# Output projection of a hybrid decoder block: four parts of 512-column matmuls in place of two sweeps of 256-column matmuls

## The chip, the cores and the metric

The kernel runs on one core of a Trainium2 chip. The metric is the device time of one execution in microseconds (us); lower is better. TensorE (PE) multiplies matrices, VectorE (DVE), ScalarE (ACT) and GpSimd (POOL) do the rest, and SyncE (SP) issues nearly all DMA transfers, one after the other, from one queue.

## The reference

One decoder layer over 2048 tokens of width 1024: a norm, one input projection, three branches that read it, and one output projection that is added to the input. Widths: attention 512 (8 heads of 64), SSD 1024 (16 heads, two groups), LRU 512. All in float32.

```python
u = rms_norm(h, norm_g[l])
proj = jnp.einsum('bsd,de->bse', u, w_in[l])
(q, k, v, z_att, f_raw, z_ssd, xbc, dt_raw, x_lru, z_lru) = jnp.split(proj, split_points, axis=-1)
y_att = fox_attention(...) * jax.nn.silu(z_att)     # causal softmax with a forget bias
y_ssd = ssd_mixer(...)                              # its RMS norm: per token and group of 512
y_lru = rglru_mixer(...) * jax.nn.silu(z_lru)
mix = jnp.concatenate([y_att, y_ssd, y_lru], axis=-1)        # 512 + 1024 + 512 = 2048
h = h + jnp.einsum('bse,ed->bsd', mix, w_out[l])             # (2048 x 2048) by (2048 x 1024)
```

## The kernel before, in words

Every large product is made of three matmuls: both operands are split into a high part (fp32r) and the rest, and high x high, high x low and low x high are summed in PSUM. So weights are loaded ("wr", "wor"), copied to a high tile by ACT, and the low tile is made by VectorE as the difference.

The stages follow one another, and the framework's scheduler fixes at build time the order of instructions on each engine and on SP's queue, from each instruction's priority (its place in the program, moved up inside `high_priority`) and its own estimate of when operands and buffers are ready. `issue_after(x)` keeps the instructions of a block behind x on the same engine.

1. u, the normed and transposed input, is kept in SBUF split (`uh`, `ul`: four blocks tb of 512 tokens, 8 + 8 tiles of 2 KB per partition each, 128 KB in all). Projections of x/B/C, LRU, z and the SSD scan run first; branch outputs go to DRAM (`gt_d` for SSD, `lr_d` for LRU).
2. For four pairs of heads: Q and K are projected and normed, then `group_vz` projects V and the attention gate, eight steps t2 of two token tiles, 48 matmuls of 256 columns each. Three PSUM banks ("pj") hold their results. After the last pair, the pools of this phase, u among them, are closed (`pb.close()`), and the pools of the next phase take their place in SBUF and PSUM.
3. Attention: 64 units (head h, block sb of 256 queries). Heads 0 and 7 go from the longest block down, the others up. `logits` makes S = QK (L814, L815), VectorE subtracts the bias and keeps a running maximum (L816), ACT takes the exponential (L820). `attend` transposes the weights (T, L869) for each pair of key tiles, ACT and VectorE split them (ph L876, pl L877), and TensorE multiplies by V (O, L855, L856). Logits of the next unit are made within the present one. There are 288 transposition steps in all, and after each, `fill` takes steps of another job, the output projection, from a generator: `count * 512 // 288` steps so far, each allowed on TensorE after the transposition LAG = 4 steps back.
4. Output projection in two sweeps over 16 row tiles t. `load_wo` loads eight row tiles of w_out (512 KB each) and splits them in pieces of 512 columns: 16 pieces on ACT and VectorE. The first sweep takes w_out's rows 8 to 15 (SSD group 1 and LRU) and goes over t upwards, the second rows 4 to 7 (SSD group 0) and 0 to 3 (attention) and goes downwards. `mix(t)` loads the branch outputs of one tile ("mt"), makes "mh" on ACT (L956, for attention after four transposes px, L948) and "ml" on POOL (L957; for attention VectorE, L949); it is called a whole tile ahead. For each quarter n of 256 columns a PSUM tile `po` of two halves, one for each part, takes 8 x 3 matmuls of 256 columns (L977, L979, L981), with a `yield` ahead of each three: 16 x 4 x 8 = 512 steps a sweep. VectorE then adds each half to "xr" (L985, scaled for SSD by its norm `rsn`; L988), and xr is stored after two quarters.

The first sweep is the filler of attention: it reads x and writes the sum to `pt_d` in DRAM, with one PSUM bank (psP). The second sweep begins after attention, with five banks for `po` and three for px; it reads `pt_d` and writes the output. Weights of both sweeps have a pool of their own, 64 KB per partition: the first set is loaded after u's pools are closed, the second set after the filler's last step.

Of the kernel before, what the change touches and what calls it, by code (L numbers as in the profile page):

```python
# [29 lines left out]
QB = 5  # L30
ZPOOL = True
# [13 lines left out]
def hybrid_block(ctx, tc, x, norm_g, w_in, q_norm_g, k_norm_g, forget_b, ssd_conv_w, ssd_conv_b,  # L45
# [110 lines left out]
    up = pb.enter_context(tpool(name="up", bufs=1))  # L156
# [147 lines left out]
    def proj_tok2(w, t2, name, space=None):  # L304
# [3 lines left out]
        for i in range(2):  # L308
            t = t2 * 2 + i
            h, l, sl = uh[t // 4], ul[t // 4], slice(t % 4 * P, t % 4 * P + P)  # L310
            for k in range(KD):
                T.matmul(ps[:, i, :], h[k][:, sl], wh[k], start=(k == 0), stop=False)  # L312
                T.matmul(ps[:, i, :], h[k][:, sl], wl[k], start=False, stop=False)  # L313
                T.matmul(ps[:, i, :], l[k][:, sl], wh[k], start=False, stop=(k == KD - 1))  # L314
        return ps

# [11 lines left out]
    def group_vz(pool, vpool, p):  # L328
# [4 lines left out]
        for t2 in range(8):  # L333
# [5 lines left out]
            else:  # L339
                pss = [proj_tok2(w, t2, f"pvz{p}_{t2}")]  # L340
            m = 2 // len(pss)
# [386 lines left out]

    with tpool(name="ap", bufs=2) as pool, tpool(name="ap1", bufs=1) as ap1, \
            tpool(name="qkp", bufs=QB) as qkp:  # L730
        for p in range(4):
# [39 lines left out]
            if p == 2:  # L771
                load_head(0)
                load_q(*units[0])
    pb.close()
# [3 lines left out]
    o2 = cx.enter_context(tpool(name="o2", bufs=2))  # L778
    a2 = cx.enter_context(tpool(name="a2", bufs=2))
    a3 = cx.enter_context(tpool(name="a3", bufs=3))  # L780
    wo = cx.enter_context(tpool(name="wo", bufs=1))
    o1 = cx.enter_context(tpool(name="o1", bufs=1))
# [120 lines left out]
    def load_wo(ks):  # L903
        w = {}
        for j, k in enumerate(ks):
            h = wo.tile([P, D], F32R, name=f"woh{k}", tag=f"woh{j}")
            l = wo.tile([P, D], F32R, name=f"wol{k}", tag=f"wol{j}")
            row = w_out[k * P:(k + 1) * P, :]
            if j < 7:
                whole = wo.tile([P, D], F32, name=f"wor{k}", tag=f"wol{j + 1}")  # L910
                dma(whole, row)
            for n in range(2):
                cs = slice(n * 512, n * 512 + 512)
                if j < 7:
                    raw = whole[:, cs]
                else:
                    raw = o1.tile([P, 512], F32, name=f"wor{k}_{n}", tag=f"mt{n}")
                    dma(raw, row[:, cs])
                if 4 <= k < 12:
                    g = c1("sg", k - 4)  # L920
                    A.activation(h[:, cs], raw, AF.Copy, scale=g)
                    V.scalar_tensor_tensor(l[:, cs], raw, g, h[:, cs].bitcast(F32),
                                           op0=ALU.mult, op1=ALU.subtract)
                else:
                    A.copy(h[:, cs], raw)
                    V.tensor_tensor(l[:, cs], raw, h[:, cs].bitcast(F32),
                                    op=ALU.subtract)
            w[k] = (h, l)
        return w

    def sweep(w, psP, psX, parts, resid, dst, ts):


        ks = [k0 + i for _, k0 in parts for i in range(4)]

        def mix(t):
            tsl = slice(t * P, (t + 1) * P)
            mh = o2.tile([P, 8, P], F32R, name=f"mh{t}_{ks[0]}", tag="mh")
            ml = o2.tile([P, 8, P], F32R, name=f"ml{t}_{ks[0]}", tag="ml")
            for j, (kind, k0) in enumerate(parts):  # L940
                sl = slice(j * 4, j * 4 + 4)
                mt = o1.tile([P, 4, P], F32, name=f"mt{t}_{k0}", tag=f"mt{j}")
                if kind == "att":
                    dma(mt.rearrange("p i c -> p (i c)"), at_d[tsl, :])
                    src = psX.tile([P, 4, P], F32, name=f"px{t}_{k0}", tag="X")
                    for i in range(4):
                        T.transpose(src[:, i, :], mt[:, i, :], ident)  # L947
                    A.copy(mh[:, sl, :], src)  # L948
                    V.tensor_tensor(ml[:, sl, :], src, mh[:, sl, :].bitcast(F32), op=ALU.subtract)  # L949
                    continue  # L950
                if kind == "lru":
                    for m in range(4):
                        dma(mt[:, m, :], lr_d[m][:, tsl])
                else:
                    dma(mt, gt_d[kind][:, :, tsl].rearrange("i p t -> p i t"))
                A.copy(mh[:, sl, :], mt)  # L956
                G.tensor_tensor(ml[:, sl, :], mt, mh[:, sl, :].bitcast(F32), op=ALU.subtract)  # L957
            return mh, ml

        cur = mix(ts[0])  # L960
        for i, t in enumerate(ts):
            nxt = mix(ts[i + 1]) if i + 1 < NT else None
            tsl = slice(t * P, (t + 1) * P)
            mh, ml = cur
            for n in range(4):
                cs = slice(n * 256, n * 256 + 256)
                if n % 2 == 0:
                    xr = o2.tile([P, 512], F32, name=f"xr{t}_{n}_{ks[0]}", tag="xr")
                    dma(xr, resid[tsl, n * 256:n * 256 + 512])
                xc = xr[:, n % 2 * 256:n % 2 * 256 + 256]  # L970

                ps = psP.tile([P, 2, 256], F32, name=f"po{t}_{n}_{ks[0]}", tag="P")
                for j, k in enumerate(ks):
                    yield
                    h, l = w[k]
                    o = ps[:, j // 4, :]
                    T.matmul(o, mh[:, j, :], h[:, cs], start=(j == 0), stop=False,  # L977
                             skip_group_check=True)
                    T.matmul(o, mh[:, j, :], l[:, cs], start=False, stop=False,  # L979
                             skip_group_check=True)  # L980
                    T.matmul(o, ml[:, j, :], h[:, cs], start=False, stop=(j % 4 == 3),  # L981
                             skip_group_check=True)
                for j, (kind, _) in enumerate(parts):
                    if kind in (0, 1):
                        V.scalar_tensor_tensor(xc, ps[:, j, :], rsn[:, t, kind:kind + 1], xc,  # L985
                                               op0=ALU.mult, op1=ALU.add)
                    else:
                        V.tensor_tensor(xc, xc, ps[:, j, :], op=ALU.add)  # L988
                if n % 2:
                    dma(dst[tsl, n * 256 - 256:n * 256 + 256], xr)  # L990
            cur = nxt

    with tc.high_priority(offset=HP):
# [3 lines left out]
    w = load_wo(range(8, 16))  # L997
    filler = sweep(w, psP, None, ((1, 8), ("lru", 12)), xf, pt_d, range(NT))
# [54 lines left out]
```

## Time and profile before

| | |
|---|---|
| three runs | 2081.85, 2084.37, 2092.38 us (median 2084.37) |
| the profiled execution | 2094.4 us, its span 2092.4 us |
| TensorE busy | 2011.2 us (96%), mean granted clock 0.985 |
| VectorE, ACT, POOL busy | 61%, 46%, 26% |
| output projection, first sweep | first matmul at 1306.7 us, fills attention |
| attention | from about 1275 to 1893 us |
| output projection, second sweep | 1898 us to the end |
| DMA | 248.59 MB, mean 119 GB/s |

Times within the execution are counted from the span's start. A row of stretches gives busy microseconds of each engine in that stretch and, in brackets, how many instructions; "PEclk" is the share of full TensorE clock that was granted. A row of the order of time gives start and duration of an instruction, and in square brackets how long its engine had been idle before it and who released it. Bars of consecutive matmuls overlap, so their durations do not add up to time.

### The profile page before, as it was taken

To read this page: it belongs to the slowest core of one execution; us is meant where nothing else is said; L and a number is where in the kernel's file an instruction comes from. 1 tells how busy PE (TensorE), PEld (TensorE's weight loads), DVE (VectorE), ACT (ScalarE), POOL (GpSimd) and SP (SyncE) were. 2 spreads that over 40 slices of the span, in tenths; PEclk is the share of its full clock that TensorE was granted. 3 is DMA by queue.
4 is the path that set the end of the run, shared out by engine and by line. 5 is a ranking of instruction groups with operands and counts; after the bars stand their busy time and mean duration, and the time that the engine had idled before them with its cause. 6 is when DMAs were issued, how large, how long until landed. Compare 5 with 4: busy or idle time off the path is not lost. (4 is left out here: it accounts for less than half of the span.)

```text
span 2092.4 us, 38943 instructions
## 1 busy us (share of the span) xinstructions
PE 2011.2 (96%) x14021; PEld 1838.4 (88%) x14021; DVE 1278.1 (61%) x2844; ACT 954.3 (46%) x1985; POOL 542.0 (26%) x750
## 2 busy tenths in 40 slices
PE   7999999999999999998999998999999999998999
PEld 6788888887789998887888996989999999997999
DVE  6654555488874226767576245677787787774333
ACT  8444443466642215454444234566556565652100
POOL 0000001355531004454552001342233323121110
PEclk9999999999999999999999999999999999998999
DMA  5122233111123225666655636365435535234443
GB/s 195 41 71 61 71 112 93 42 42 42 42 72 98 82 80 165 188 182 197 190 166 177 167 116 205 100 165 144 116 110 147 132 105 155 64 100 139 137 133 106
DMA packets 277826, 248.59 MB, mean 119 GB/s; under 512 B 58725, under 2 KB 225153, under 8 KB 275585
## 3 DMA queue, kind: packets, MB, share of 16 engines
q1 hardware_dynamic: 277472, 246.07, 40.6%
q8 instruction: 111, 1.82, 0.4%
q0 software_dynamic: 160, 0.03, 0.1%
q14 instruction: 83, 0.67, 0.1%
HBM read 159.83 MB, written 86.18 MB: 118 GB/s over the span
## 5 line engine op out<-in xcount | busy, mean ns | idle before, releaser
L977 PE MATMUL po<-woh,mh 128*128 128x256 f32 x1024 | 295.2, 289 | 7.3 <-ACT mh L956 7.3
L981 PE MATMUL po<-woh,ml 128*128 128x256 f32 x1024 | 289.3, 283 | 0.0
L979 PE MATMUL po<-wol,mh 128*128 128x256 f32 x1024 | 288.2, 282 | 0.0
L876 ACT CAST ph<-T 128x512 fp32r<-128x512 f32 (+2 forms) x352 | 163.4, 490 | 144.4 <-PE T L869 79.7
L877 DVE TENSOR_TENSOR pl<-T,ph 128x512 fp32r<-128x512 f32 (+2 forms) x352 | 191.0, 563 | 32.5 <-ACT ph L876 32.2
L977 PEld LDWEIGHTS po<-woh,mh 128*128 128x128 f32 x1024 | 193.8, 189 | 10.4 <-ACT mh L956 8.0
L979 PEld LDWEIGHTS po<-wol,mh 128*128 128x128 f32 x1024 | 194.4, 190 | 2.7
L981 PEld LDWEIGHTS po<-woh,ml 128*128 128x128 f32 x1024 | 193.4, 189 | 1.0
L820 ACT ACTIVATE L<-L,mx 128x1920 f32<-128x1920 f32 (+15 forms) x128 | 154.7, 1209 | 54.6 <-DVE mx L819 39.0
L869 PE MATMUL T<-ident,L 128*128 128x128 f32 x1088 | 175.6, 276 | 1.2 <-ACT L L820 0.8
L373 DVE SCALAR_TENSOR_TENSOR accx<-rtx,cv,accx 128x512 f32<-128x512 f32 x144 | 104.6, 752 | 90.4 <-ACT accx L370 76.2
L855 PE MATMUL O<-ph,vv 128*128 128x256 f32 x576 | 154.7, 288 | 3.0 <-ACT ph L876 3.0
L322 PE MATMUL pxx<-uh,wh 128*128 128x512 f32 x384 | 152.7, 400 | 4.7 <-ACT rtx L365 3.3
L856 PE MATMUL O<-pl,vv 128*128 128x256 f32 x576 | 154.1, 291 | 1.0 <-DVE pl L877 0.9
L323 PE MATMUL pxx<-ul,wh 128*128 128x512 f32 x384 | 153.4, 400 | 0.0
L313 PE MATMUL pqk<-wl,uh 128*128 128x256 f32 x512 | 152.6, 299 | 0.8 <-DVE wl L187 0.8
L324 PE MATMUL pxx<-uh,wl 128*128 128x512 f32 x384 | 152.3, 398 | 0.0
L312 PE MATMUL pqk<-wh,uh 128*128 128x256 f32 x512 | 147.8, 293 | 3.0 <-ACT wh L186 3.0
L809 POOL TENSOR_SCALAR_AFFINE_SELECT cm<-cb 128x384 f32<-128x384 f32 (+3 forms) x128 | 58.7, 460 | 352.8 <-DVE mx L816 229.9
L314 PE MATMUL pqk<-wh,ul 128*128 128x256 f32 x512 | 149.5, 294 | 0.0
L313 PE MATMUL pzs<-wl,uh 128*128 128x256 f32 x512 | 144.5, 284 | 3.2 <-POOL wl L187 3.2
L314 PE MATMUL pzs<-wh,ul 128*128 128x256 f32 x512 | 144.4, 283 | 0.0
(313 smaller groups left out, 5661.2 us busy)
## 6 DMA issues: line engine op xcount, KB each, us to landing
ab<-acs_d SPq DMA_DIRECT2D x64, 256.0 KB
wr<-in_w_in_dram SPq DMA_DIRECT2D x192, 64.0 KB
wr<-in_w_in_dram SPq DMA_DIRECT2D x80, 128.0 KB
xt<-in_x_dram SPq DMA_DIRECT2D x16, 512.0 KB
xs_d<-stx SPq DMA_DIRECT2D x32, 256.0 KB
v_d<-vs SPq DMA_DIRECT2D x32, 256.0 KB
zs_d<-zs SPq DMA_DIRECT2D x32, 256.0 KB
xs<-xs_d SPq DMA_DIRECT2D x32, 256.0 KB
```

What stands on the lines that cost most here:

```text
L313: T.matmul(ps[:, i, :], h[k][:, sl], wl[k], start=False, stop=False)
L314: T.matmul(ps[:, i, :], l[k][:, sl], wh[k], start=False, stop=(k == KD - 1))
L323: T.matmul(ps, wh[k][:, ms], ul[tb][k], start=False, stop=False)
L820: A.activation(lt[:, 0:n], lt[:, 0:n], AF.Exp, bias=mx, accum_out=sm[:, i:i + 1])
L855: T.matmul(po[:, ca], vv[:, kt, :], ph[:, jj, ca], start=(kt == 0), stop=False)
L856: T.matmul(po[:, ca], vv[:, kt, :], pl[:, jj, ca], start=False, stop=(kt == nk - 1))
L869: ins = T.transpose(pt[:, jj, i * P:(i + 1) * P], L[i][:, kt * P:(kt + 1) * P], ident)
L876: A.copy(ph[:, ja, ca], pt[:, ja, ca])
L877: V.tensor_tensor(pl[:, ja, ca], pt[:, ja, ca], ph[:, ja, ca].bitcast(F32), op=ALU.subtract)
L977: T.matmul(o, mh[:, j, :], h[:, cs], start=(j == 0), stop=False, skip_group_check=True)
L979: T.matmul(o, mh[:, j, :], l[:, cs], start=False, stop=False, skip_group_check=True)
L981: T.matmul(o, ml[:, j, :], h[:, cs], start=False, stop=(j % 4 == 3), skip_group_check=True)
```

## The change

- **Parts.** The output projection is done in four parts of four row tiles of w_out: rows 12 to 15 (LRU), 8 to 11 (SSD group 1), 4 to 7 (SSD group 0), 0 to 3 (attention). One matmul covers 512 columns, `po` is one bank of 512 columns for one part, and one VectorE instruction of 512 columns adds it. A part has 16 x 2 x 4 = 128 steps of three matmuls, all four parts 512.
- **Passes over the sum.** Part one reads x and writes `pt_d`, part two reads and writes `pt_d`. Parts three and four are chained: for each t, part three loads `pt_d` into a tile "xo" of 1024 columns (three buffers), and part four, LEAD = 3 tiles later, adds to it there and stores the output. Both go downwards over t.
- **Weights.** Their tiles are slots of u's own first half: blocks tb 0 and 1 now have a pool of their own (`upa`) that lives on, blocks 2 and 3 another (`upb`) that is closed as before. A part's weights fill one block (32 KB per partition). The first two parts' weights are loaded in the program ahead of `pb.close()`; those of part three into tb 0's place after part one, those of part four into tb 1's after part two, both inside the filler.
- **Start.** The logits of unit 0, at raised priority, are now also kept behind the last matmul of step t2 = 4 of the last `group_vz` (`anchor`). FIRST = 12 steps of the filler stand in the program ahead of unit 0's `attend`.
- **Rate and end.** `fill` takes `12 + count * 260 // 288` steps, 272 by the end of attention: parts one and two (256 steps) and 16 of part three. The remaining 240 follow with five banks for `po` and three for px. `mix` of the next item is called halfway through the present one, and mixes of the attention part only after attention's PSUM pools are closed.

```diff
-    up = pb.enter_context(tpool(name="up", bufs=1))
+    upa = ctx.enter_context(tpool(name="upa", bufs=1))
+    upb = pb.enter_context(tpool(name="upb", bufs=1))
...
+        up = upa if tb < 2 else upb
...
+    def load_wo(k0, half, lastp, tag):
+        ws = {}
+        pl = [(k0 + i, n) for i in range(4) for n in range(2)]
+        tags = [f"u{p}{half}_{k}" for k in range(KD) for p in "hl"]
+        for j, (k, n) in enumerate(pl):
+            h = upa.tile([P, 512], F32R, name=f"woh{k}_{n}", tag=tags[2 * j])
+            l = upa.tile([P, 512], F32R, name=f"wol{k}_{n}", tag=tags[2 * j + 1])
...
+            if j + 1 < len(pl):
+                raw = [upa.tile([P, 512], F32, name=f"wor{k}_{n}", tag=tags[2 * j + 3])]
+            else:
+                raw = [lastp.tile([P, 256], F32, name=f"wor{k}_{n}_{i}", tag=tag) for i in range(2)]
...
+    ws = [load_wo(12, 0, wrp, "wr"), load_wo(8, 1, wrp, "wr")]
     pb.close()
...
+    def half(t, n, i, parts, xr):
+        k0, kind = SEQ[i]
+        mh, ml = parts
+        ps = pso["P"].tile([P, 512], F32, name=f"po{t}_{n}_{k0}", tag="P")
+        for j in range(4):
+            yield
+            h, l = ws[i][k0 + j, n]
+            T.matmul(ps, mh[:, j, :], h, start=(j == 0), stop=False)
+            T.matmul(ps, mh[:, j, :], l, start=False, stop=False)
+            T.matmul(ps, ml[:, j, :], h, start=False, stop=(j == 3))
+        if kind in (0, 1):
+            V.scalar_tensor_tensor(xr, ps, rsn[:, t, kind:kind + 1], xr, op0=ALU.mult, op1=ALU.add)
+        else:
+            V.tensor_tensor(xr, xr, ps, op=ALU.add)
+
+    SEQ = ((12, "lru"), (8, 1), (4, 0), (0, "att"))
+
+    def sweeps():
+        for i in range(2):
+            cur = mix(0, *SEQ[i])
+            for t in range(NT):
+                nxt = mix(t + 1, *SEQ[i]) if t + 1 < NT else None
...
+                for n in range(2):
+                    xr = o2.tile([P, 512], F32, name=f"xr{t}_{n}_{i}", tag="xr")
+                    dma(xr, (pt_d if i else xf)[tsl, cs])
+                    yield from half(t, n, i, cur, xr)
+                    dma(pt_d[tsl, cs], xr)
+                cur = nxt
+            ws.append(load_wo(SEQ[i + 2][0], i, o2, "mt"))
+        xs = {}
+        work = [(t, 2) for t in range(LEAD)]
+        for t in range(NT):
+            work.append((t, 3))
+            if t + LEAD < NT:
+                work.append((t + LEAD, 2))
+        work = [(NT - 1 - t, i) for t, i in work]
+        cur = mix(work[0][0], *SEQ[2])
+        for w, (t, i) in enumerate(work):
+            if i == 2:
+                xs[t] = o3.tile([P, D], F32, name=f"xo{t}", tag="xo")
+                dma(xs[t], pt_d[tsl, :])
+            if i == 3 and cur is None:
+                cur = mix(t, *SEQ[3])
+            nxt = None
+            for n in range(2):
+                if n == 1 and w + 1 < len(work) and (work[w + 1][1] == 2 or "X" in pso):
+                    nxt = mix(work[w + 1][0], *SEQ[work[w + 1][1]])
+                yield from half(t, n, i, cur, xs[t][:, cs])
+                if i == 3:
+                    dma(of[tsl, cs], xs[t][:, cs])
+            cur = nxt
...
-    with tc.high_priority(offset=HP):
+    with tc.high_priority(offset=HP), tc.issue_after(anchor[1].ins):
         cur, steps = logits(*units[0])
...
-    w = load_wo(range(8, 16))
-    filler = sweep(w, psP, None, ((1, 8), ("lru", 12)), xf, pt_d, range(NT))
-    count = [0, 0]
+    filler = sweeps()
+    for _ in range(FIRST):
+        next(filler)
+    count = [0, FIRST]
...
-        want = count[0] * 512 // 288
+        want = FIRST + count[0] * RATE // 288
```

More of the change, by code (lines that the diff above doesn't have):

```diff
@@ L30 @@
 QB = 5
+FIRST = 12
+RATE = 260
+LEAD = 3
 ZPOOL = True
@@ L313, in proj_tok2 @@
                 T.matmul(ps[:, i, :], h[k][:, sl], wl[k], start=False, stop=False)
-                T.matmul(ps[:, i, :], l[k][:, sl], wh[k], start=False, stop=(k == KD - 1))
+                ins = T.matmul(ps[:, i, :], l[k][:, sl], wh[k], start=False, stop=(k == KD - 1))
+        anchor[0] = ins
         return ps
+    anchor = [None, None]
     def proj_ch(w, m, tb, name):
@@ L340, in group_vz @@
                 pss = [proj_tok2(w, t2, f"pvz{p}_{t2}")]
+                if p == 3 and t2 == 4:
+                    anchor[1] = anchor[0]
             m = 2 // len(pss)
@@ L901, in hybrid_block, with mix @@
     pt_d = dram("pt_d", [S, D])
[L903 to L911, printed above, removed]
+    pso = {"P": psP}
+    def mix(t, k0, kind):
+        tsl = slice(t * P, (t + 1) * P)
+        mh = o2.tile([P, 4, P], F32R, name=f"mh{t}_{k0}", tag="mh")
+        ml = o2.tile([P, 4, P], F32R, name=f"ml{t}_{k0}", tag="ml")
+        mt = o2.tile([P, 4, P], F32, name=f"mt{t}_{k0}", tag="mt")
+        if kind == "att":
+            dma(mt.rearrange("p i c -> p (i c)"), at_d[tsl, :])
+            src = pso["X"].tile([P, 4, P], F32, name=f"px{t}_{k0}", tag="X")
+            for i in range(4):
+                T.transpose(src[:, i, :], mt[:, i, :], ident)
+            A.copy(mh, src)
+            V.tensor_tensor(ml, src, mh.bitcast(F32), op=ALU.subtract)
+            return mh, ml
+        if kind == "lru":
+            for m in range(4):
+                dma(mt[:, m, :], lr_d[m][:, tsl])
+        else:
+            dma(mt, gt_d[kind][:, :, tsl].rearrange("i p t -> p i t"))
+        A.copy(mh, mt)
+        G.tensor_tensor(ml, mt, mh.bitcast(F32), op=ALU.subtract)
+        return mh, ml
@@ L928, in load_wo @@
[L928 to L990, printed above, removed]
```

47 lines of the change are left out of this document (24 added, 23 removed).

## The prediction

> **What bounds the kernel now.** I read the page's shares first, then stretches of 10 us around both ends of attention, then the order of time on TensorE, then groups by line and shape.
>
> ```profile
> span 2092.4 us, 38943 instructions
> PE 2011.2 (96%) x14021; PEld 1838.4 (88%) x14021; DVE 1278.1 (61%) x2844; ACT 954.3 (46%) x1985; POOL 542.0 (26%) x750
> ```
>
> TensorE is busy for 96% of the span, so time can be won in two ways only: by less work on it, or by closing its 81 us of gaps. The next rows say where gaps are. Columns after the stretch: its length, busy us of PE (count), PEld, DVE, ACT, POOL, then the granted clock, DMA share, GB/s.
>
> ```profile
> 1270.00:1280.00 10.00, 8.36 (x57) 6.67 (x55) 5.34 (x16) 3.61 (x7) 0.30 (x1) 1.00 0.70 218
> 1280.00:1290.00 10.00, 6.74 (x25) 4.40 (x24) 9.83 (x24) 9.53 (x16) 1.35 (x2) 0.75 1.03 391
> 1290.00:1300.00 10.00, 8.03 (x45) 5.69 (x44) 10.00 (x24) 6.38 (x12) 2.80 (x4) 0.91 1.06 252
> 1300.00:1310.00 10.00, 6.10 (x40) 5.04 (x39) 5.49 (x16) 5.55 (x10) 4.25 (x6) 0.94 0.63 160
> 1310.00:1320.00 10.00, 10.00 (x61) 9.55 (x62) 4.76 (x14) 5.92 (x11) 3.86 (x6) 0.72 0.21 60
> ...
> 1360.00:1370.00 10.00, 10.00 (x84) 9.78 (x84) 7.36 (x31) 6.40 (x22) 6.30 (x11) 1.00 1.03 259
> 1370.00:1380.00 10.00, 7.45 (x51) 5.76 (x50) 7.19 (x30) 5.85 (x17) 5.01 (x12) 1.00 0.80 202
> ```
> ```profile
> 1880.00:1890.00 10.00, 4.15 (x17) 2.84 (x15) 9.14 (x20) 10.00 (x24) 4.56 (x6) 0.78 0.78 290
> 1890.00:1900.00 10.00, 4.00 (x17) 3.42 (x18) 4.75 (x9) 1.67 (x4) 2.72 (x4) 0.50 0.32 92
> 1900.00:1910.00 10.00, 10.00 (x76) 10.00 (x76) 2.92 (x6) 1.79 (x3) 1.31 (x1) 0.86 0.38 107
> ```
> ```profile
> 1400.00:1870.00 470.00, 468.89 (x3654) 445.62 (x3653) 367.55 (x1083) 280.72 (x547) 136.12 (x264) 1.00 0.44 117
> ```
>
> Between 1400 and 1870 us TensorE idles for 1.1 us in 470 while VectorE is at 78%: the middle of attention is bound by TensorE. At the start of attention (1270 to 1320) it idles 1.64 + 3.26 + 1.97 + 3.90 = 10.8 us, and its clock falls. Work done at a clock of c loses (1 - c) of its time, so 0.25 x 6.74 + 0.09 x 8.03 + 0.06 x 6.10 + 0.28 x 10 = 5.6 us go that way. Together **16.4 us are lost at the start**. At the end (1880 to 1910) it is 5.85 + 6.00 = 11.9 us idle, and 0.22 x 4.15 + 0.50 x 4.00 + 0.14 x 10 = 4.3 us by the clock: **16.2 us at the end**. What ended these gaps:
>
> ```profile
> 1303.79 0.28 PE L855 MATMUL O<-ph,vv 128*128 128x256 f32 x1
> 1306.65 0.38 PE L977 MATMUL po<-woh,mh 128*128 128x256 f32 x1 [2.59 <-ACT mh L956]
> ```
> ```profile
> 1892.69 0.69 PE L893 MATMUL pf<-ident,os 128*128 128x128 f32 x2 [0.52 <-ACT os L889]
> 1898.12 0.58 PE L977 MATMUL po<-woh,mh 128*128 128x256 f32 x1 [4.74 <-ACT mh L956]
> ```
> ```profile
> 1272.54 0.92 SPq L911 DMA_DIRECT2D wor<-in_w_out_dram  x2
> ```
>
> Output projection is the only work that needs no softmax, and at both ends it isn't there yet: its first matmul comes at 1306.65 and that of the second sweep at 1898.12, both behind mh. At the start the weights' loads are issued only at 1272.54, and their splitting then keeps VectorE at 9.83 and 10.00 of 10 us.
>
> **The change, part by part.**
>
> *1. Matmuls of 512 columns in place of 256.* 3072 of 256 columns become 1536 of 512. Bars of one matmul overlap, so the price is the step from start to start. The first two rows are the ends of 28 matmuls of 512 in a row, the next two of 64 of 256:
>
> ```profile
> 199.71 0.40 PE L323 MATMUL pxx<-ul,wh 128*128 128x512 f32 x1
> ...
> 205.96 0.40 PE L323 MATMUL pxx<-ul,wh 128*128 128x512 f32 x1
> ```
> ```profile
> 1267.71 0.28 PE L314 MATMUL pvz<-wh,ul 128*128 128x256 f32 x1
> ...
> 1275.17 0.28 PE L314 MATMUL pvz<-wh,ul 128*128 128x256 f32 x1
> ```
>
> 6.25 / 27 = 0.2315 us and 7.46 / 63 = 0.1184 us. Two narrow ones cost 0.2368, one wide one 0.2315; 1536 x 0.0053 = **8.2 us saved**, all on the bound engine. The mean durations in the groups (289 and 400 ns) would promise 1536 x 0.178 = 273 us and are the wrong column. The Trainium skill ("TensorE: Matmul & The Clock Gate", Back-to-back issue gap) puts one warm matmul at 262 cycles for 256 columns and 518 for 512, at 2.4 GHz; that is a fixed 2.5 ns each, and the saving would be 1536 x 2.5 ns = 3.8 us and the time 2060 in place of 2055. The rows here stand above its 109 and 216 ns, so the trace's steps are taken.
>
> *2. Start of attention.* The first weights go into the first half of u. Its two token quarters are last read by the last V/Z group, a quarter being two of eight equal steps that end at 1275.17; each step is 48 matmuls x 0.1184 = 5.7 us, so the quarters come free near 1241 and 1252. Loading (4.2 MB) and splitting then lie beside matmuls that leave ACT and VectorE mostly free, and the 16 splits on VectorE leave the start:
>
> ```profile
> L922 DVE SCALAR_TENSOR_TENSOR wol<-wor,cv,woh 128x512 fp32r<-128x512 f32 x16 | 11.8, 765 | 1.1 <-ACT woh L921 1.1
> L926 DVE TENSOR_TENSOR wol<-wor,woh 128x512 fp32r<-128x512 f32 x16 | 10.5, 694 | 0.1
> ```
>
> That is 8 x 0.765 + 8 x 0.694 = 11.7 us off VectorE where it is saturated. FIRST puts 12 steps of 3 x 0.2315 = 0.694 us, 8.3 us of TensorE work, ahead of the first unit. What stays: mt and mh lie in u's last quarter, free only after 1275.17, and the way from a load's issue to the first matmul is
>
> ```profile
> 1894.45 0.41 SPq L955 DMA_DIRECT2D mt<-gt_d  x1
> ```
> ```profile
> 1897.45 0.62 ACT L956 CAST mh<-mt 128x512 fp32r<-128x512 f32 x1 [4.81 <-DMA mt<-gt_d]
> ```
>
> with the 1898.12 above, 3.7 us; the first part loads in four pieces, so near 5 us. Logits and transposes of unit 0 cover part. Bounds of the loss that stays: 0 and the whole 16.4. I take 4, nearer this row than the old gap: **12 us saved**. The SP queue issues the 17 new loads among the V/Z stores, and the hoisted logits wait for the anchor matmul; both stand beside 5.7 us steps with three PSUM banks, so zero, and if that cover is gone it is the first rival.
>
> *3. End of attention.* Weights of the last two parts are loaded and split inside attention (after steps 128 and 256), 16 of their 256 steps run before its end, and the rest can start as logits' banks come free. No load of weights or first mix stands between; what stays is the latency of the last small units, 2 us of 16.2 taken (bounds 0 and 16.2): **14 us saved**.
>
> *4. What attention pays.* Two bursts, 8 x 0.765 = 6.1 and 8 x 0.694 = 5.6 us on VectorE, and 16 splits on ACT, now fall into the TensorE-bound stretch. By the sum they fit: 470 - 367.55 = 102 us are free, and accumulating gets cheaper:
>
> ```profile
> L985 DVE SCALAR_TENSOR_TENSOR xr<-po,rsn,xr 128x256 f32<-128x256 f32 x128 | 61.6, 481 | 123.8 <-PE po L981 123.8
> L988 DVE TENSOR_TENSOR xr<-xr,po 128x256 f32<-128x256 f32 x128 | 53.4, 418 | 2.6
> L277 DVE SCALAR_TENSOR_TENSOR ul<-pu,ngc,uh 128x512 fp32r<-128x512 f32 x32 | 23.0, 745 | 12.9 <-ACT uh L276 12.6
> L646 DVE TENSOR_TENSOR y<-py,xs 128x512 f32<-128x512 f32 x32 | 21.9, 684 | 8.7 <-PE py L642 5.7 <-POOL st L665 2.6 <-issue 0.3
> ```
>
> 64 x (0.481 + 0.418) = 57.5 us in attention become 36 x 0.745 + 32 x 0.684 = 48.7. In the moment a burst delays pl and so the O matmuls; fills held back by four steps cover some 4 x 0.63 us. Bounds 0 and 11.7, taken **4 us**. The partial sum is written and read once more: 2 x 8.4 MB over some 600 us, 28 GB/s on top of 117, which takes the DMA share from 0.44 to some 0.55, and 64 more issues stand on SP's queue, where the fetches of q, za and the stores of attention wait behind them. 117 GB/s cost TensorE 1.1 us in 470; I take **1 us** more; the upper end is in the third rival.
>
> *5. The chained end.* 240 of 512 steps remain, 240 x 0.694 = 167 us. The old pace, from one tile to the next, shows no gap (96 x 0.1184 + four transposes):
>
> ```profile
> 1925.07 1.31 POOL L957 TENSOR_TENSOR ml<-mt,mh 128x512 fp32r<-128x512 f32 x1 [10.43 <-ACT mh L956]
> 1936.82 1.31 POOL L957 TENSOR_TENSOR ml<-mt,mh 128x512 fp32r<-128x512 f32 x1 [10.44 <-ACT mh L956]
> ```
>
> New is that xo has three buffers: 13 times a load must wait for the store of the tile three before it.
>
> ```profile
> SPq L969 <- DMA out_dram<-xr: 51.5, 30, 3.4
> ```
>
> Add 0.7, store up to 3.4, load 3.0 (as mt above) or a little more: some 7 us after an item ends, while its successor's first sum is ready after 4 x 0.694 = 2.8 us. Only the sum waits; five PSUM banks hold 13.9 us of matmuls, so zero on TensorE. If that cover is gone, it is the last rival. Of the mixes, the load of gt_d is issued a tile ahead:
>
> ```profile
> 1926.40 0.37 SPq L955 DMA_DIRECT2D mt<-gt_d  x1
> ```
>
> ten us before its product is used at 1936.82; I expect buffers, not the place in the program, to set it again.
>
> **The sum.** -8.2 - 12 - 14 + 4 + 1 = **-29.2 us**. The profiled execution took 2094.4 us (span 2092.4), 10.0 above the median of the three runs, 2084.37; the same 29.2 off the median gives **2055**, and a span near 2063 if the profile falls as high again.
>
> **The rivals.**
>
> *The start isn't filled* (15%). Weights come late because the loads are still issued behind the V/Z stores, as at 1272.54. For it: SP works in order, and the fills' mix lies in u's last quarter. Against: the new tiles are slots of u's own pool, free from 1241. Time: 2055 + 12 = 2067.
>
> *The bursts land on TensorE in full* (12%). For it: where splits and logits met (1280 to 1300), VectorE was full and TensorE idle. Time: 2055 + 11.7 - 4 = 2063.
>
> *Attention gives it back to the transfers* (10%). After the DMA share of 1.03 at 1360 TensorE idled 2.55 us. Seven heads are fetched in attention; if the added 28 GB/s makes each cost 2.55 more, 17.9 us go: 2073, at the limit of no change. Against: the other heads' fetches lie in the 470 us that lost 1.1.
>
> *Slower* (6%): on SP's queue the mix of the next item stands behind the load of xo that waits for a store. It then issues 4 us after an item ends and its matmul starts 3.7 to 5 us later, at 8 to 9 us, not 5.6; 13 x 3.3 = 43 us, 2098. It decides from 29.2 / 13 = 2.2 us a pair. Against: the mix is loaded a whole item earlier, as the 1926.40 row suggests.
>
> **The numbers.** The forecast has 57%, and the time is its: 2055. Low end: everything at its best, 8.2 + 16.4 + 16.2 = 41 us, 2043, less 3 for the median's own spread (2081.85 to 2092.38). High end: the third rival, 2073, and as much spread, 2076. A measurement of this kernel tells about 0.5% (10 us) from no change: faster is below 2074. The forecast, the first two rivals, and some of the third count as faster: 0.85; same 0.09; slower 0.06.
>
> **What would show it.** Right: 1536 po matmuls of 512 at steps of 0.23 us; splits of the first weights before 1275; TensorE idle under 4 us between 1270 and 1320 and under 3 us at the end; 0.99 busy in the chained part. Wrong: weight splits after 1275, PE idle after a burst on VectorE, waits for px or mh in the last 170 us, or a middle of attention that is longer than the 605 us between 1275 and 1880 by more than the 7 us of moved steps.

## The result, and the profile after

The changed kernel takes 2097.38 us (median of six runs, 2093.96 to 2099.9) against 2084.4 for the kernel before: a ratio of 1.0060, interval 1.0040 to 1.0079. It is slower by 0.6%, where 2055 and faster was forecast. Its profiled execution is its fastest, 2093.96 us. That of the kernel before (2094.4) was 10 us above its own median, so two spans that look alike, 2092.4 and 2092.3, belong to medians 13 us apart. For a fair base the kernel before was profiled once more (2082.32 us, span 2080.4); "before" means that second execution from here on, unless the first is named.

The page of the changed kernel, totals of each engine:

```profile
span 2092.3 us, 35912 instructions
PE 2008.3 (96%) x12485; PEld 1760.1 (84%) x12485; DVE 1261.7 (60%) x2720; ACT 956.7 (46%) x1989; POOL 540.6 (26%) x750
```

There are 1536 matmuls fewer and no less time. Four stretches around attention, in the columns of the prediction (length, then busy us of PE, PEld, DVE, ACT, POOL; clock, DMA share, GB/s). First the kernel before in its second execution, then the changed one:

```profile
1270.00:1320.00 50.00, 40.60 (x265) 33.22 (x264) 38.93 (x98) 32.31 (x55) 12.94 (x17) 0.97 0.78 229
1320.00:1400.00 80.00, 77.39 (x609) 73.23 (x609) 58.83 (x193) 45.84 (x106) 28.07 (x57) 1.00 0.51 140
1400.00:1870.00 470.00, 468.89 (x3656) 445.74 (x3655) 367.53 (x1086) 280.94 (x549) 137.42 (x268) 1.00 0.42 116
1870.00:1930.00 60.00, 48.34 (x366) 46.40 (x366) 28.82 (x63) 18.21 (x40) 11.20 (x12) 0.83 0.50 163
```
```profile
1270.00:1320.00 50.00, 41.98 (x236) 34.67 (x235) 25.70 (x70) 19.93 (x32) 10.52 (x16) 0.93 0.71 197
1320.00:1400.00 80.00, 76.38 (x483) 67.65 (x482) 57.83 (x182) 45.76 (x106) 29.65 (x59) 0.96 0.60 166
1400.00:1870.00 470.00, 454.54 (x2870) 396.19 (x2870) 351.73 (x990) 273.60 (x527) 131.22 (x253) 0.99 0.53 147
1870.00:1930.00 60.00, 56.37 (x332) 47.40 (x331) 38.41 (x104) 28.41 (x67) 17.48 (x29) 0.97 0.34 96
```

Loss is idle time plus (1 - clock) of the busy time, as in the prediction. In the order of the rows it was 10.6, 2.6, 1.1 and 19.9 us before, and is 11.0, 6.7, 20.0 and 5.3 after: 34.2 against 43.0. The end was won (19.9 to 5.3). The start, 1270 to 1320, was not. The middle, the second and third row, went from 3.7 to 26.7; of these, 3.7 and 19.1 are idle time. (The clock is given to two digits, which over 470 us can hide some 2 us: by rows of 10 us the 26.7 would be 25.5.) The whole is 8.7 us more loss, and the spans differ by 11.9.

Four of the larger gaps after, in the order of time on TensorE (start, duration, then in brackets the idle time and its releaser), and, second, what VectorE did there:

```profile
1303.29 0.80 PE L977 MATMUL po<-woh,mh 128*128 128x512 f32 x1 [6.21 <-DVE xr L983]
1376.21 0.66 PE L933 MATMUL pf<-ident,os 128*128 128x128 f32 x2 [3.33 <-DVE ats L934]
1539.16 0.50 PE L854 MATMUL S<-kh,qh 128*128 128x512 f32 x1 [2.00 <-DVE mx L856]
1762.94 0.51 PE L977 MATMUL po<-woh,mh 128*128 128x512 f32 x1 [2.49 <-DVE xr L981]
```
```profile
1302.55 0.69 DVE L983 TENSOR_TENSOR xr<-xr,po 128x512 f32<-128x512 f32 x1 [8.14 <-DMA xr<-in_x_dram]
1375.64 0.42 DVE L934 TENSOR_REDUCE ats<-pf 128x128 f32<-128x256 f32 x1 [4.72 <-DMA at_d<-ats]
1537.95 0.42 DVE L934 TENSOR_REDUCE ats<-pf 128x128 f32<-128x256 f32 x1 [3.80 <-DMA at_d<-ats]
1762.13 0.75 DVE L981 SCALAR_TENSOR_TENSOR xr<-po,rsn,xr 128x512 f32<-128x512 f32 x1 [2.65 <-DMA xr<-pt_d]
```

Each of these TensorE gaps ends within 1.3 us of a row on VectorE that had itself waited for a transfer. TensorE's row at 1539.16 names mx, an ordinary step of the softmax. The cause stands one row earlier in VectorE's order: it takes its instructions one after another, and the reduction into ats, with two buffers, had to wait until an older ats was stored. mx, pl and the sums stood behind it. By the view of waits, from 1270 to 1870 VectorE stands for transfers for these totals (us, times, longest), the first row in the second execution of the kernel before, the next three after:

```profile
DVE ats L894 <- DMA at_d<-ats: 2.7, 1, 2.7
```
```profile
DVE ats L934 <- DMA at_d<-ats: 14.5, 4, 4.7
DVE xr L983 <- DMA xr<-in_x_dram: 8.1, 1, 8.1
DVE xr L981 <- DMA xr<-pt_d: 2.6, 1, 2.6
```

SP's queue, too, stands for buffers. For the load of xr, which waits for the store of the half two before it, it stands 79.2 us between 1320 and 1870, against 27.8 in the first execution of the kernel before:

```profile
SPq L969 <- DMA pt_d<-xr: 27.8, 23, 2.1
```
```profile
SPq L996 <- DMA pt_d<-xr: 79.2, 49, 5.9
```

### The profile page after: what moved, and what is told of

Read it like the earlier page. It is cut to its first block, busy times and chain, and to the rows that moved or that the text cites. A ratio compares the mean times of both kernels' runs of the same rounds, so it can differ in the third digit from the quotient of the medians.

```text
span 2092.3 us, 35912 instructions
## 1 busy us (share of the span) xinstructions
PE 2008.3 (96%) x12485; PEld 1760.1 (84%) x12485; DVE 1261.7 (60%) x2720; ACT 956.7 (46%) x1989; POOL 540.6 (26%) x750
## 5 line engine op out<-in xcount | busy, mean ns | idle before, releaser
L977 PE MATMUL po<-woh,mh 128*128 128x512 f32 x512 | 215.3, 421 | 9.4 <-DVE xr L983 6.2
L978 PE MATMUL po<-wol,mh 128*128 128x512 f32 x512 | 202.9, 396 | 0.0
L979 PE MATMUL po<-woh,ml 128*128 128x512 f32 x512 | 201.3, 398 | 0.0
L318 PE MATMUL pzs<-wh,uh 128*128 128x256 f32 x512 | 143.3, 283 | 0.0
L648 ACT ACTIVATE ab<-ab,nacs 128x128 f32<-128x128 f32 x256 | 82.6, 391 | 129.9 <-POOL ab L644 115.2
L854 PE MATMUL S<-kh,qh 128*128 128x512 f32 (+2 forms) x320 | 130.3, 408 | 10.8 <-DVE mx L856 10.1
```

What stands on the lines that cost most here:

```text
L977: T.matmul(ps, mh[:, j, :], h, start=(j == 0), stop=False)
L978: T.matmul(ps, mh[:, j, :], l, start=False, stop=False)
L979: T.matmul(ps, ml[:, j, :], h, start=False, stop=(j == 3))
```

## The experiments

Three theories. **A**: two buffers of xr and two of ats are too few for the transfers as they now run; VectorE stands in order behind a late one. **B**: steps of 0.69 us in place of 0.36 hide a unit's softmax chain less well. **C**: the weight splits inside attention cost it. Lines of code below are of the changed kernel. All ratios are against the kernel before; the changed kernel stands at 1.0060. They compare with runs of the kernel before from the same set, whose median lay between 2081.0 and 2084.4 us, so kernels are compared by their ratios, not their medians. The waits are those of VectorE for transfers at its rows of ats and of parts one and two's sums from 1270 to 1870, whatever transfer the view names for them.

| kernel | ratio, 95% interval | median, us | VectorE's waits at ats / at xr or xw, us | PE idle, 1270 to 1930, us |
|---|---|---|---|---|
| before | 1 | 2084.4 | 2.7 / 0 | 24.8 |
| changed | 1.0060 (1.0040 to 1.0079) | 2097.4 | 14.5 / 10.9 | 30.7 |
| more buffers, both | 0.9916 (0.9897 to 0.9936) | 2065.3 | 0 / 0.7 | 15.2 |
| xr alone | 0.9997 (0.9982 to 1.0012) | 2082.0 | 18.8 / 2.5 | 24.4 |
| ats alone | 1.0015 (0.9999 to 1.0032) | 2087.0 | 0 / 10.0 | 25.2 |
| part one without its transfers | 0.9978 (0.9962 to 0.9994) | 2077.0 | 5.9 / 1.6 | 17.6 |
| no fetch of heads 2 to 7 | 0.9940 (0.9919 to 0.9961) | 2071.5 | 0 / 9.0 | 19.4 |
| fetch of a head in four parts | 1.0076 (1.0055 to 1.0098) | 2097.2 | 17.5 / 8.6 | 32.8 |
| stores of ats from GpSimd | 0.9994 (0.9972 to 1.0016) | 2081.7 | 14.6 / 11.4 | 27.2 |
| finer steps | 1.0069 (1.0044 to 1.0093) | 2099.6 | 22.4 / 9.7 | 38.5 |
| more buffers, finer steps | 0.9957 (0.9943 to 0.9971) | 2073.5 | 0 / 0.7 | 19.9 |
| before, 512 columns alone | 1.0005 (0.9990 to 1.0020) | 2083.2 | 3.5 / 0 | 23.8 |
| more buffers, part three's weights a piece a tile | 0.9961 (0.9941 to 0.9981) | 2075.6 | 0 / 2.7 | 21.4 |

**1. More buffers.**

```diff
-        ats = a2.tile([P, 2, 64], ...)             # two buffers
+        ats = o4.tile([P, 2, 64], ...)             # four
+                xw = o3.tile([P, D], F32, ..., tag="xo")     # three tiles of 1024 columns
-                    xr = o2.tile([P, 512], F32, ..., tag="xr")   # two of 512
+                    xr = xw[:, cs]
```

> The changed kernel with more buffers only: parts one and two keep their residual and sum in the slots of the chained parts' tile xo (three tiles of 128x1024 in place of two of 128x512, so six halves instead of two), and ats, the attention output that waits to be stored, gets four buffers in place of two. Work, matmuls, transfers and order are those of the changed kernel. Theory A (VectorE, which takes its instructions in order, stands for a completed transfer of xr or ats while a head is fetched, and TensorE then waits for pl, mx or the sum): the waits of VectorE L934 and L981 for DMA go, the 15.5 us that TensorE idles between 1400 and 1870 fall below 6, and the time falls by 10 to 15 us against the changed kernel, to 2082 to 2088. Theory B (steps of 0.69 us in place of 0.36 cover the softmax chain of a unit less well): no wait of TensorE changes and the time stays at 2097, plus or minus 3. Theory C (the splits of weights inside attention cost it): also no change.

Measured 2065.34, a ratio of 0.9916: **0.8% faster than the kernel before**, and more than twice the 15 us that theory A had promised against the changed kernel. The same four stretches:

```profile
1270.00:1320.00 50.00, 48.35 (x276) 40.85 (x276) 32.14 (x87) 23.83 (x38) 13.09 (x21) 0.97 0.77 226
1320.00:1400.00 80.00, 77.02 (x495) 67.28 (x494) 59.55 (x187) 48.10 (x109) 29.80 (x61) 0.98 0.60 169
1400.00:1870.00 470.00, 461.27 (x2961) 404.40 (x2960) 366.63 (x1028) 284.63 (x558) 137.64 (x260) 1.00 0.53 152
1870.00:1930.00 60.00, 58.13 (x298) 48.26 (x297) 22.72 (x50) 13.11 (x33) 10.62 (x17) 1.00 0.29 94
```

Losses are 3.1, 4.5, 8.7 and 1.9, together 18.2: 24.7 less than in the changed kernel, by spans 27.2. Of VectorE's waits of 25.4 us at ats and at the sums, 0.7 is left. The expectation counted only the idle time of the middle; it left out the start (7.9 us of loss) and the clock, which is low beside some of the gaps: 0.83 in the slices of 10 us from 1570, 1690 and 1760 of the changed kernel, 3.8 us of loss, and 1.00 in the same slices here. SP's queue now stands 22.9 us in place of 81.4 (1270 to 1870).

**2. xr alone, 3. ats alone.** Each half of that diff by itself.

> The changed kernel with the residual and sum of parts one and two in the slots of xo (six halves in place of two), ats with two buffers as it was. If the buffers of xr carry what the first run with more buffers gained (32 us), this comes to 2065 to 2070; if ats carries it, it stays at 2097; if each holds a part, about 2080, with the waits of VectorE L934 for the store of ats left in the trace.

> The changed kernel with four buffers of ats in place of two, and xr with two as it was. By the trace of the changed kernel between 1400 and 1870 us VectorE stands 9.8 us for stores of ats and 2.6 us for a load of xr, so by the waits as they are named ats would carry more: 2080 to 2087. If the named wait is only the last in a queue that xr's stores and loads fill, it gains little: 2090 to 2097.

Both hold a part: by the ratios 0.63% and 0.45% of 1.44%. They mend different places. With more of xr the start is whole (48.48 of 50 us busy from 1270 to 1320), and in the middle 452.10 of 470 are busy, less than in the changed kernel. With more of ats the start is as it was (40.38) and the middle has 459.23. The kernel with xr alone also shows that SP's standing isn't what makes the stores late: it falls to 25.0 us while the waits at ats rise to 18.8. The worst one, on SP, VectorE and TensorE:

```profile
1674.29 0.38 SPq L724 DMA_DIRECT2D vv<-v_d  x1
1674.76 3.84 SPq L936 DMA_DIRECT2D at_d<-ats  x1
...
1684.04 0.42 DVE L934 TENSOR_REDUCE ats<-pf 128x128 f32<-128x256 f32 x1 [8.21 <-DMA at_d<-ats]
...
1685.31 0.79 PE L854 MATMUL S<-kh,qh 128*128 128x512 f32 x1 [7.26 <-DVE mx L856]
```

A store of 64 KB is issued right behind a head's values of 1 MB. Its issue takes 3.84 us, where others take 0.4, and it is done 9 us after it began.

**4. Part one without its transfers.**

```diff
-                    dma(xr, (pt_d if i else xf)[tsl, cs])
+                    if i:
+                        dma(xr, xf[tsl, cs])
...
-                    dma(pt_d[tsl, cs], xr)
+                    if i:
+                        dma(pt_d[tsl, cs], xr)
```

> The changed kernel without the extra pass over the partial sum: part one neither loads x nor stores its sum, part two loads x, so the contribution of part one to the output is left out; the matmuls, splits and order stay, and one copy of the bank takes the place of each sum of part one. It takes away 64 issues on SP's queue and 16.8 MB. Theory A with the transfers as its cause: in part one's stretch of attention (to about 1590) TensorE's idle time at heads falls to that of the kernel before, about 1 us, in part two's it stays; in all 6 to 10 us less than the changed kernel, 2087 to 2091. If the buffers and not the traffic are short, part two's gaps stay as they are (about 8 us). Theory B: time within 3 us of 2097.

This kernel leaves part one's contribution out of the output. 2077.0, 0.8% less than the changed kernel by the ratios, twice what was expected. In part one's stretch every wait of VectorE for a transfer is gone, the one of 8.1 us at the start with them; in part two's stretch three stay (5.4, 1.6 and 0.5 us). TensorE's idle time says the same: from 1320 to 1590 it is 11.8 us in the changed kernel, 3.5 here and 3.1 before; from 1590 to 1870, where the transfers stay, 7.3, 9.9 and 0.6.

**5. No fetch of heads 2 to 7.**

```diff
     def load_head(h):
+        if h >= 2:
+            heads[h] = heads[h - 2][:3]
+            return
```

> The changed kernel without the fetch of heads 2 to 7: they use the keys, values and bias of heads 0 and 1, so their attention is left out of the output in that form; every instruction on the engines stays, and 6 x 3 MB of transfers with 24 issues on SP go; the fetch of head 1 at the start stays. Buffers as in the changed kernel (two of xr, two of ats). If the stores of ats and the loads of xr are late because they share the transfers with a head's 3 MB, the waits of VectorE at 1462, 1538, 1694 and 1762 us go, and the time falls by 12 to 20 us, to 2077 to 2085, with the gap of 6 us at the start (head 1) left. If two buffers of xr on SP's queue are too few without any fetch, the waits stay and it is 2092 to 2097.

2071.5, a little better than expected. With two buffers of each and the second pass in place, VectorE waits only 0.2 us for transfers from 1320 to 1870:

```profile
1270.00:1320.00 50.00, 41.85 (x239) 34.74 (x238) 26.98 (x72) 19.84 (x32) 10.01 (x15) 0.93 0.70 193
1320.00:1400.00 80.00, 79.86 (x528) 71.17 (x527) 61.16 (x190) 49.04 (x111) 30.68 (x61) 1.00 0.43 132
1400.00:1870.00 470.00, 460.76 (x2945) 403.03 (x2944) 366.54 (x1030) 282.56 (x549) 134.61 (x258) 1.00 0.40 121
```

The one long wait left is of 8.0 us at the start, where head 1 is still fetched. So the waits need both, the fetch of a head and the extra pass: the fetches alone cost the kernel before 2.7 us of waits and part one's stretch in run 4 none, the pass alone costs 0.2 here. TensorE still idles 9.4 us from 1320 to 1870 (19.1 in the changed kernel, 11.7 with more buffers, 3.7 before), so not all of the middle's loss is theirs.

**6. A head's fetch in four parts**, one per unit, in place of all in one unit.

> The changed kernel with the fetch of a head (1 MB of cb, two of 0.5 MB for kh, 1 MB of vv) cut into its four transfers, one in each of four units that follow one another, in place of all in one unit; buffers as in the changed kernel. If the burst of a head's fetch is what holds back the loads of xr and the stores of ats, the gaps shrink and the time falls by 10 to 25 us, to 2072 to 2087. If the two buffers of xr are too few for the usual time of a transfer, whatever else is fetched, it stays within 5 us of 2097.

No gain: 2097.2. But the run doesn't test what it was made for, because the order on SP's queue hardly changed. The issues of a head lay apart already in the changed kernel. The first and the last of head 4, in the changed kernel and then in this one:

```profile
1508.25 0.32 SPq L721 DMA_DIRECT2D cb<-c_d  x1
1527.93 0.37 SPq L724 DMA_DIRECT2D vv<-v_d  x1
```
```profile
1511.09 0.32 SPq L722 DMA_DIRECT2D cb<-c_d  x1
1530.75 0.37 SPq L728 DMA_DIRECT2D vv<-v_d  x1
```

That is 19.7 us in both; over heads 2 to 7 it is 20 to 26 us in both kernels. So the time that stays says nothing on the text's second reading, buffers too few whatever else is fetched; run 5 shows that reading to be wrong. Smaller pieces than the half megabyte to a megabyte of these transfers were not tried.

**7. Stores of ats issued from GpSimd.**

> The changed kernel with the 64 stores of ats issued from GpSimd, which makes ats, in place of SP; buffers as in the changed kernel (two of ats, two of xr). If the stores of ats are late because SP's queue stands (79 us at loads of xr) and because they go behind a head's megabyte in SP's transfers, this frees them: VectorE's waits for stores of ats go and the time falls by about 10 us, to 2087, as with four buffers. If the transfers themselves are slow, whatever queue they are on, the waits stay, and so does 2097.

The time came out at the better end, the reason did not: VectorE's waits for these stores remain.

```profile
DVE ats L934 <- DMA at_d<-ats: 14.6, 7, 3.8
```

The queue that issues the store isn't what holds it. The Trainium skill ("DMA: Bandwidth & Descriptors", Issuing engines are not separate DMA queues) has transfers started by different engines run on the same 16 DMA engines and interleave, so that starting them on several engines saves only issue time; 14.5 and 14.6 us agree. What the 0.66% came from is not settled. The two profiles differ by 3.5 us of TensorE's idle time and 6.5 us of span, but the one of this kernel (2087.53 us) lies 5.8 above its median and that of the changed kernel 3.4 below.

**8. Finer steps, 9. more buffers and finer steps** (a yield ahead of each matmul, FIRST 36, RATE 780).

> The changed kernel with fills cut finer: each fill step is one matmul of 512 columns (0.23 us) in place of three, with three times as many steps (36 ahead of the first unit, 780 per 288 calls), so the same work is spread more evenly; nothing else changes. Theory B: TensorE's idle time in the middle of attention falls from 15.5 to below 5 us and the time by about 10 us, to 2087. Theory A: the gaps at the fetches of heads remain, time 2097 plus or minus 3.

> More buffers for both (as in the first run) and steps of one matmul in place of three. With VectorE's waits for transfers gone, the remaining 8.7 us of idle time of TensorE in the middle of attention stand behind mx, L and pl at unit boundaries. If coarse steps cause these (theory B as a second term), it gains 4 to 7 us against 2065, to 2058 to 2061; if not, 2065 plus or minus 3.

Finer steps gain nothing by themselves, and with more buffers they are 0.4% slower, 2073.5 against 2065.3. But the finer steps of the program did not become finer on TensorE: from 1400 to 1870 us an unbroken series of the projection's matmuls has 4.3 on average (12 at most) in the changed kernel, and 4.4 (11 at most) with finer steps. So these runs don't decide on theory B. Run 1 does: it keeps the coarse steps and is faster than the kernel before, so they are not the main cause, and run 10 gives their price. Why the second of these runs is slower is not settled; its profile is that of its slowest execution (2080.75). The largest gap there is again an engine in order behind a transfer, here ACT at the weights of part three:

```profile
1556.44 0.72 ACT L760 ACTIVATE woh<-wor,cv 128x512 fp32r<-128x512 f32 x1 [4.48 <-DMA wor<-in_w_out_dram]
...
1558.77 1.54 PE L910 MATMUL T<-ident,L 128*128 128x128 f32 x6 [4.88 <-ACT L L861]
```

**10. The kernel before with 512 columns alone.**

> The kernel before with matmuls of 512 columns alone: both sweeps, their weights in one place, the start and the end of attention stay, a bank of 512 holds one part after the other, and there are 256 fill steps of three wide matmuls in place of 512 of three narrow ones. By the prediction's first term it is 8.2 us faster than before, 2076 (by a step of 0.227 us as the chained part of the changed kernel shows it, 15 us, 2069). Theory B: the coarse steps cost the middle of attention about 10 us, so it comes out at 2076 to 2087 with TensorE idle at unit boundaries between 1400 and 1870. Theory A: the middle stays at about 1 us of idle time.

2083.2, no change. In the second sweep the pace of the tiles tells why. From one tile to the next, 96 narrow or 48 wide matmuls and four transposes, first in the kernel before (second execution), then in this one:

```profile
1918.97 1.31 POOL L957 TENSOR_TENSOR ml<-mt,mh 128x512 fp32r<-128x512 f32 x1 [10.02 <-ACT mh L956]
1930.30 1.30 POOL L957 TENSOR_TENSOR ml<-mt,mh 128x512 fp32r<-128x512 f32 x1 [10.02 <-ACT mh L956]
```
```profile
1929.64 1.31 POOL L957 TENSOR_TENSOR ml<-mt,mh 128x512 fp32r<-128x512 f32 x1 [10.13 <-ACT mh L956]
1941.08 1.31 POOL L957 TENSOR_TENSOR ml<-mt,mh 128x512 fp32r<-128x512 f32 x1 [10.13 <-ACT mh L956]
```

11.33 us narrow, 11.44 wide. The prediction's row pair had 11.75, from the first execution. In the first sweep it is otherwise. By all its rows from 1400 to 1870 the median step from one of its matmuls to the next is 118 ns narrow, in both executions of the kernel before, and 229 ns wide, so a pair of narrow ones costs 7 ns more, and 768 pairs some 5 us. That gain is nearly eaten: in the same stretch TensorE is busy for 465.01 us, where it was 468.89 before, so 3.9 us more are idle. This is theory B's part, and it is small.

**11. More buffers, part three's weights loaded and split a piece a tile.**

> More buffers for xr and ats as in the first run, and the weights of part three loaded and split one piece a row tile over the first eight tiles of part two, in place of all at once between parts. In the run with more buffers TensorE idles 2.33 us in three waits for mx near 1556 to 1561, where VectorE does these splits. If the burst is their cause, they go, and the time is 2 to 4 us below 2065, at 2061 to 2063; if not, 2065 plus or minus 2.

The burst was not spread. The scheduler put seven of the eight pieces together again: their splits on VectorE lie between 1550.24 and 1561.57 us, those of all eight pieces in run 1 between 1549.21 and 1561.54. From 1545 to 1570 TensorE idles 2.1 us, and 2.6 in run 1. Only the last piece moved, and the time is 10 us longer than in run 1: the piece's two loads, into slots of mt, were late, and ACT stood for them in the middle of two units, which left TensorE idle for 6.8 us. ACT, then TensorE:

```profile
1672.80 0.51 ACT L765 ACTIVATE woh<-wor,cv 128x256 fp32r<-128x256 f32 x1 [6.23 <-DMA wor<-in_w_out_dram]
1680.62 0.51 ACT L765 ACTIVATE woh<-wor,cv 128x256 fp32r<-128x256 f32 x1 [4.94 <-DMA wor<-in_w_out_dram]
```
```profile
1673.62 0.69 PE L939 MATMUL pf<-ident,os 128*128 128x128 f32 x2 [4.82 <-ACT os L935]
...
1681.44 0.44 PE L939 MATMUL pf<-ident,os 128*128 128x128 f32 x2 [1.98 <-ACT os L935]
```

So no run tests theory C. What can be read in run 1 is TensorE's idle time beside its two bursts: 2.6 us from 1545 to 1570 and 1.8 from 1840 to 1870, together 4.4, where the kernel before, without bursts there, idles less than 0.1. That the splits cause these 4.4 us is likely and not shown. The best version stays that of run 1.

**12. The kernel before, profiled again.**

> The kernel before, unchanged, for a second profile. The prediction read the losses at the two ends of attention (16.4 and 16.2 us) from one execution that took 2094.4 us, 10 above the median of its kernel. If these losses belong to every execution, they show again, and the 10 us lie elsewhere; if that execution had a bad start or end, the losses here sum to about 22 in place of 32.6, and the change had less to win.

Neither: the two ends lose 10.6 and 19.9 us here by the rows above, 30.5 together, and 16.3 and 18.6 by the same rows of the first execution. The start was 5.6 us worse there, and the second sweep ran at 11.75 us a tile in place of 11.33, 16 x 0.42 = 6.7 us. Together that is nearly all of the 12.0 us between the spans, with the end 1.3 us better to set against it.

## Why the prediction was wrong, step by step

- **Step 4, what attention pays: this is the step that failed.** It took 4 us for the bursts and 1 for "64 more issues on SP's queue" and the extra pass. The bursts can be what it took (4.4 us of idle time beside them in run 1, cause not shown). The term of 1 us was far too small: the middle of attention loses 26.7 us where it lost 3.7, more buffers alone win back 13.5 of the 23.0 there and 7.9 at the start, and without the fetch of heads 2 to 7 17.3 are won back in the middle. The 9.5 us that stay with more buffers are about the idle time beside the bursts (4.4) and what run 10 shows of coarse steps (3.9). The prediction named the place, q, za and the stores of attention behind the new issues, and then priced it from a mean (DMA share 0.44, 1.1 us lost in 470). What mattered wasn't the mean but a coincidence of three: two buffers of each, a second pass that brings more transfers and, with a tile of xr in use for four wide steps in place of sixteen narrow ones, gives each of its turns half the time, and a head's 3 MB. Runs 1, 4 and 5 each take away one of the three, and each takes the waits with it where it applies; the shorter turn by itself was not tested.
- **The rival of the transfers was the mechanism.** It had the head's fetch as the trigger and was sized at 2.55 us for each of seven heads, 2073. Run 5 measured the fetch of six heads at 1.2% of the time between the ratios, some 25 us, 4 us a head, among it idle gaps of 1.6 to 3.3 us in five places and, in three slices, the clock of 0.83. Its counter-argument, that the other heads' fetches cost 1.1 us in 470, held for the kernel before and said nothing on a kernel with half the time per buffer.
- **Step 2, the start.** Its own parts came true: weights split by 1268.6 us, first fill at 1280.53. The loss is 11.0, not 4. The step went through mt, mh and SP's order of the weights, and not through xr, whose third load was issued behind head 1's fetch at 1294.14 and landed at 1302.5. With more buffers the loss is 3.1, within the step's 4. It was also priced against 16.4 us of loss, of which 5.6 belonged to that one execution.
- **Step 1, the width.** 8.2 us expected, none measured in time (run 10, interval 0.9990 to 1.0020). The difference of 5 ns a pair that the two rows showed is there in the first sweep (7 ns by the medians of run 10), and idle time of coarser steps takes most of it back, which the step put at nothing. In the second sweep it depended on the execution: the narrow step was 118 ns in the first and 113 in the second, so the wide tiles of run 10 were 0.31 us faster than the one's and 0.11 slower than the other's. The Trainium skill ("TensorE: Matmul & The Clock Gate", Back-to-back issue gap) would give the wide ones 3.8 us, by a fixed 2.5 ns a matmul; the second sweep's tiles, 11.33 against 11.44 us, don't show it.
- **Step 3, the end**: right. 14 expected, 14.6 by the rows (19.9 to 5.3), and 1.9 left with more buffers where 2 was taken.
- **Step 5, the chained end**: right. VectorE waited 27.1 us there for loads of xo, and TensorE was busy for all of 1930 to 2050; the rival on SP's queue order did not come. That its time, 2098, lies beside the measured 2097.4 is chance: it had the loss behind attention, and the loss was in it.
- **The base.** The working took terms from one execution and subtracted them from a median 10 us lower. Of the 12 us that this execution lost against the second one, 5.6 at the start were counted as winnable and weren't there to be won in others; the 6.7 of the second sweep's pace no term claimed.

The kernel of run 1 is what the sum described, without the width and without these 5.6 us: -29.2 + 8.2 + 5.6 = -15.4. By its losses it is 16.0 us better than the kernel before (34.2 to 18.2), by the spans 15.3. That it fits so well is in part luck: the end gave 18.0 us where 14 were taken, and the middle cost 9.5 where 5 were.

## What to carry to other kernels

When work is cut finer, ask of every buffer how long one turn now lasts and what is the longest time that its transfer takes, not the mean: here a head's 3 MB set it, and a store behind one megabyte of it took 9 us. An engine that works in order turns one late store into a stall for everything behind it, so a row that names an ordinary step (mx, pl, L) sends the reader one row back on that engine. Profile the base twice before terms of a few microseconds are taken from it. And look in the trace whether an edit took place on the engines: those of runs 6, 8, 9 and 11 changed the program and hardly the order on the engines, so their times say little on what they were made for.

## What was not expected of the hardware

The same instructions ran at two paces with a granted clock of 1.00 in the rows of both: 11.75 and 11.33 us for a chained tile of the kernel before, 3.7% apart, each steady from 1920 to 2030 us. Until 1870 the median step of the narrow matmuls was 118 ns in both executions; in the second sweep it stayed at 118 in the first and was 113 in the second. No view showed what differs; it stays open. And an issue on SP isn't always short: behind a head's fetch one took 3.84 us, and one 9.24 us in the kernel with more buffers, which hid it:

```profile
1288.52 9.24 SPq L998 DMA_DIRECT2D xw<-in_x_dram  x1
```
